# Gate and up of 19 weight tiles in two feed-forward layers: seven products of halves with sums on VectorE, in place of eight products

## The chip, the cores and the metric

The kernel runs on one core of a Trainium2 chip. The metric is the device time of one launch in microseconds (us); lower is better.

## What is computed

The reference is a diffusion backbone of two blocks over 256 context and 256 latent tokens of width 1024. Each block is a feed-forward layer, a mixer and a second feed-forward layer, so there are four feed-forward layers; the kernel's loops call them 0 to 3 by their order. The last one works on the latents alone. A feed-forward layer is, in short:

```python
def _swiglu_sub(x, mod, j, g_pre, g_post, w_in, w_out):
    h = _modulate_pre(x, g_pre, mod[:, 3 * j], mod[:, 3 * j + 1])
    gate, up = jnp.split(h @ w_in, 2, axis=-1)
    y = (jax.nn.silu(gate) * up) @ w_out
    return _gated_post(x, y, g_post, mod[:, 3 * j + 2], FFN_RES)
```

`w_in` is 1024 x 5632 (2816 columns of gate, 2816 of up), `mod` is the conditioning vector's product with `w_mod`. In the text below, "layers 2 and 3" are the second and the third feed-forward layer in the order in which they run: the last of block 0 and the first of block 1. Both work on all 512 tokens.

## The kernel before

**Numbers as two parts.** Every fp32 operand of a product is split exactly into a high part (type fp32r, made by ScalarE with a Copy) and a low part (the rest, made by VectorE with a subtraction). A product is then three matmuls: high by high, high by low, low by high. h lies in `hhi` and `hlo`, transposed, with 1024 features as eight k tiles on the partitions and the 512 tokens as columns.

**Weights.** A weight tile `f` (0 to 21) holds 128 columns of gate and 128 of up for all 1024 features: 1 MB, one DMA into one of two buffers `wraw`, then `whi` on ScalarE (L501) and `wlo` on VectorE (L502), each 128 x 2048, in three buffers each. `chunk` keeps two tiles ahead.

**The layer.** `ffn` runs the first three tiles stream by stream (`first`), since the second stream's h becomes ready later: 256 tokens at a time, gate and up in one PSUM bank (`split`). For tiles 3 to 21 (`rest`) both streams go together: 24 matmuls of 512 columns for gate, 24 for up (L656 to L658), then Silu on ScalarE (L761) and the product with up on VectorE (L762) into `act`. Behind each tile stands some modulation work (`mods`): with rate 1.75, one or two jobs, each a 512 KB load and, per stream that needs it, one pass of VectorE over 1024 columns with an accumulator (L541). Then `out_proj` multiplies `act`, split in two parts once more (L861, L862), with `w_out` in eleven chunks; its last chunks go token tile by token tile, and behind each token tile come the norms (L584 to L619) and the transposes and parts of the next layer's h (L633 to L648).

**Order.** TensorE and POOL run in the order of the program; for VectorE, ScalarE and SP (which issues the DMAs) a scheduler sets the order when the kernel is built. Every engine works through its own queue in order. `mods` puts its passes behind the last product of the tile.

Of the kernel before, what the change touches and what calls it, by code (L numbers as in the profile page):

```python
# [29 lines left out]
def rev(t):  # L30
    """128 chunk columns in the order of the backward scan: 63..0, 127..64."""
    st = t.ap[-1][0]
    return bass.AP(tensor=t.tensor, offset=t.offset + 63 * st,
                   ap=[list(x) for x in t.ap[:-1]] + [[64 * st, 2], [-st, 64]])
# [6 lines left out]
class S5Prep:  # L41
    """Discretised parameters of all 16 x 2 state groups, put down in DRAM per pair of groups."""
# [86 lines left out]
    def angles(self):  # L129
        """Everything of size [128, 16 = (dir, pair)]: first the phasors."""  # L130
# [7 lines left out]
        # phasor of one chunk, conjugated: exp(-4 i theta)  # L138
# [7 lines left out]
    def phasors(self):  # L146
        """exp(-4 i theta 2^k), k = 0..6"""
        self.steps = [self.ph]
        for k in range(1, 7):
            br, bi = self.new(), self.new()  # L150
            self.cmul(br, bi, *self.steps[k - 1], *self.steps[k - 1])
            self.unit(br, bi)
            self.steps.append((br, bi))

    def small(self, r4):
        """then the coefficients; r4 outlives the preparation"""
# [9 lines left out]
        # powers, by (pair, dir, i): forward i = power, backward i = 4 - power  # L166
# [30 lines left out]
        # input coefficients: forward j takes power 3 - j, backward j takes power j  # L197
# [8 lines left out]
    def table(self, d, q0, pool):  # L206
        """Phasor powers 0..127 of four pairs, by doubling."""
# [25 lines left out]
    def zero(self, pool):  # L233
        self.bd = pool.tile([128, 2, 2, 4, 2, 16], F32, name="s5bd", tag="s5mid", bufs=1)   # ri, dir, j, g, ch
# [4 lines left out]
    def pair(self, q, pool):  # L239
# [4 lines left out]
        B = [self.bc[:, q, :, k, :] for k in range(4)]            # [128, dir, 16]: b_re, b_im, c_re, c_im  # L244
# [27 lines left out]
    def pair_pe(self, q, pool):  # L272
# [12 lines left out]
        # by lag: the second direction's alone, both at lag 0, the first one's alone  # L285
# [19 lines left out]
class S5Main:  # L305
    """States and read-out; columns of u4 are chunks of four tokens, context first."""
# [23 lines left out]
    def fill(self, mt, ps, s=None):  # L330
        """u4 of the four pairs whose channels lie in ps [128, 512 (or one stream's 256) tokens]."""
# [94 lines left out]
# the start: feature tiles whose scale the tensor engine makes; those whose latents' scale goes by way of Pool  # L426
PE_SCALE, POOL_SCALE = 3, (3, 4, 5, 6)
# weight tile f is loaded behind the modulation of START_LOAD[f], its halves converted at feature tile 2 f, 2 f + 1
START_LOAD = (1, 3, 5)

class Kern:
# [6 lines left out]
    # ---------------------------------------------------------------- pools  # L440
# [28 lines left out]
    def ps(self, name, hold=None):  # L469
        """the next PSUM bank; hold: a set that keeps it from being given again until let() is called"""  # L470
# [11 lines left out]
    # ---------------------------------------------------------------- weights  # L482
# [3 lines left out]
    def load_upto(self, n, into=None, pieces=1, pool=False):  # L486
        """Have the n next chunks of the order on their way: raw, then its two exact parts."""
# [18 lines left out]
    def chunk(self, ahead=2):  # L506
        """The next chunk to be used."""
# [7 lines left out]
    def warm(self, f):  # L515
        """have the table of an activation function loaded"""
        self.nc.scalar.activation(self.junk_a[:, 0:1], self.mh[:, 0:1], f)

    # ---------------------------------------------------------------- modulation
# [5 lines left out]
    def mods(self, n):  # L525
        """modulation work, not before the last swiglu"""
# [25 lines left out]
    def scale_cols(self, layer, j, streams):  # L552
        """A = g_pre * (1 + scale)"""
# [6 lines left out]
    def gate_rows(self, layer, j, weight, streams):  # L560
        """weight * gate * g_post of each stream, the same row on all partitions."""
# [19 lines left out]
    # ---------------------------------------------------------------- norms  # L581
    def rstd2(self, ss):
        """ss[2] = (ss[0] + ss[1] + eps) ** -0.5"""
# [3 lines left out]
    def rstd(self, ms, n=1):  # L587
        """(ms + eps) ** -0.5 in place"""
# [4 lines left out]
    def post(self, t, y, gg, store=False):  # L593
        """x += rms(y) * gg for token tile t; y: two PSUM halves"""
# [13 lines left out]
    def pre(self, t, tag="xn"):  # L608
        """normalised token tile"""
# [12 lines left out]
    def pre_t(self, toks, layer, j):  # L622
        """h transposed, in two parts, for one or two token tiles of a stream"""
# [15 lines left out]
    def h_parts(self, p, s, k, tok, layer, j, on_vector):  # L639
        """the two parts of feature tile k of h from its transposed normalised tokens p"""  # L640
# [9 lines left out]
    # ---------------------------------------------------------------- products  # L650
    def mm_w_stat(self, out, hi, lo, col, sl):
        """out = W[:, col : col + 128].T @ h over 8 k tiles; W [128, 8, 256]"""
        nc = self.nc
        for k in range(8):
            w1, w2 = hi[:, k, col:col + 128], lo[:, k, col:col + 128]
# [4 lines left out]
    def mm_a_stat(self, outs, ahi, alo, whi, wlo, first, last):  # L660
        """outs[i] += a.T @ w[i] for one k tile; a [128, 128], w halves"""
# [7 lines left out]
    def out_proj(self, n_chunks, parts, toks, finish, tail=3):  # L669
        """token-major y = a @ W with a's k tiles on partitions; W in chunks of two k tiles.  # L670
        parts(c) -> (hi, lo) [128, 2, tokens]; the last chunks go token tile by token tile."""
# [11 lines left out]
        # the last chunks go token tile by token tile; of four tiles, the last two side by side, which  # L683
        # lets go of the chunks one by one
# [32 lines left out]
        self.bank = bank        # the banks of the first token tiles are free again first  # L717
# [4 lines left out]
    # ---------------------------------------------------------------- sub-layers  # L722
    def boundary(self, layer, j, weight, streams, nxt):
        """finish(t, y) for out_proj: post-norm of (layer, j), then the next sub-layer's pre-norm;
        nxt: (layer, j, streams), whose transposes h_ready() puts into the tensor engine's order"""
# [867 lines left out]
```

## Time and profile before

| | us |
|---|---|
| median of 3 runs | 1696.23 (1695.68 to 1696.50) |
| profiled execution, first to last instruction (the span) | 1695.7 |
| TensorE busy | 1613.1 |
| VectorE busy | 1072.1 |
| ScalarE busy | 597.6 |

The profile gives the profiled execution's span and no other time of it; it lies 0.5 us below the median of the runs. Busy time counts an engine's instructions, with overlapping ends counted once. The profile calls the engines PE (TensorE), DVE (VectorE), ACT (ScalarE), POOL and SP; PEclk is TensorE's granted clock as a share of 2.4 GHz. A line number is one of the kernel before, unless the text says that it is one of the changed kernel.

### The profile page before, as it was taken

The page shows a single profiled execution, that of the slowest core. Times are in us where ns is not written, and L with a number is a line of the kernel's source. Part 1 is how long each engine was busy: PE and PEld are TensorE (multiplying, and loading weights), DVE is VectorE, ACT ScalarE, POOL GpSimd, SP SyncE. Part 2 cuts the span into 40 slices and gives each one's busy share as a digit, 9 for nine tenths or more (in the row PEclk, how much of TensorE's full clock was granted, in tenths as well). Part 3 has the DMA queues.
Part 4 walks back from the last instruction along what each step waited for, and adds up shares of the span by engine and source line. Part 5 has one row for each costly group of instructions (what it writes and reads, how often), then busy time and mean ns, then how long its engine had stood idle before and what let it go on. Part 6 is the DMA issues. An engine that isn't in the chain of part 4 may idle for free.

```text
span 1695.7 us, 21390 instructions
## 1 busy us (share of the span) xinstructions
PE 1613.1 (95%) x8260; PEld 1358.0 (80%) x8260; DVE 1072.1 (63%) x1938; ACT 597.6 (35%) x895; POOL 268.9 (16%) x405
## 2 busy tenths in 40 slices
PE   5799959999988999999999999999999998999998
PEld 4587848888877789888888888888888877889986
DVE  6999377777657975866667465544323377665454
ACT  4431122322563444222222243222222255664342
POOL 3448800000126511000000010000000023410000
PEclk9899979999999999999999999999999999999999
DMA  7335265554342432644455422655322232135452
GB/s 307 133 125 208 90 217 183 176 218 183 119 150 97 162 136 100 224 186 186 170 180 209 162 100 105 231 186 181 112 106 99 100 115 100 63 125 199 178 208 99
DMA packets 56533, 263.93 MB, mean 156 GB/s; under 512 B 6432, under 2 KB 10992, under 8 KB 36848
## 3 DMA queue, kind: packets, MB, share of 16 engines
q1 hardware_dynamic: 56432, 262.57, 42.5%
q8 instruction: 65, 1.06, 0.2%
q14 instruction: 36, 0.29, 0.1%
HBM read 254.12 MB, written 8.43 MB: 155 GB/s over the span
## 4 chain that ended last, share of the span: by engine, by line
PE 73%; DVE 6%; POOL 3%; ACT 3%; issue 2%; POOLq 0%; DVEq 0%; ACTq 0%
PE y L667 9%; PE y L665 9%; PE y L664 9%; PE g L658 5%; PE g L656 5%; PE u L658 5%; PE g L657 5%; PE u L657 5%; PE u L656 5%; PE gu L656 3%; PE gu L658 3%; PE gu L657 3%; DVE wlo L502 1%; ACT whi L501 1%; ACT u L338 1%
## 5 line engine op out<-in xcount | busy, mean ns | idle before, releaser
L501 ACT ACTIVATE whi<-wraw 128x2048 fp32r<-128x2048 f32 (+1 forms) x155 | 285.8, 1846 | 405.7 <-PE u L657 219.7
L502 DVE TENSOR_TENSOR wlo<-wraw,whi 128x2048 fp32r<-128x2048 f32 x147 | 337.3, 2295 | 120.6 <-ACT whi L501 120.3
L541 DVE SCALAR_TENSOR_TENSOR junkv<-mraw,cond 128x1024 bf16<-128x1024 f32 x224 | 273.6, 1221 | 50.7 <-DMA mraw<-wmod 48.7
L664 PE MATMUL y<-whi,ahi 128*128 128x512 f32 x616 | 243.7, 396 | 0.0
L665 PE MATMUL y<-wlo,ahi 128*128 128x512 f32 x616 | 243.0, 394 | 0.0
L667 PE MATMUL y<-whi,alo 128*128 128x512 f32 x616 | 198.3, 395 | 0.0
L585 POOL TENSOR_TENSOR ssy<-ssy,mh 128x1 f32<-128x1 f32 x20 | 11.1, 553 | 1129.7 <-DVE ssy L584 1129.7
L658 PE MATMUL g<-hhi,wlo 128*128 128x512 f32 x456 | 179.8, 394 | 0.9 <-DVE wlo L502 0.9
L658 PE MATMUL u<-hhi,wlo 128*128 128x512 f32 x456 | 179.4, 393 | 0.0
L657 PE MATMUL g<-hlo,whi 128*128 128x512 f32 x456 | 179.1, 393 | 0.0
L657 PE MATMUL u<-hlo,whi 128*128 128x512 f32 x456 | 178.8, 392 | 0.0
L656 PE MATMUL g<-hhi,whi 128*128 128x512 f32 x456 | 178.6, 392 | 0.0
L656 PE MATMUL u<-hhi,whi 128*128 128x512 f32 x456 | 177.2, 389 | 0.0
L762 DVE TENSOR_TENSOR act<-u,act 128x512 f32<-128x512 f32 x60 | 41.4, 689 | 180.7 <-PE u L658 153.3
L657 PE MATMUL gu<-hlo,whi 128*128 128x256 f32 x496 | 139.5, 281 | 3.4 <-POOL hlo L648 3.4
L656 PE MATMUL gu<-hhi,whi 128*128 128x256 f32 x496 | 139.0, 280 | 0.0
L658 PE MATMUL gu<-hhi,wlo 128*128 128x256 f32 x496 | 138.4, 279 | 0.0
L664 PEld LDWEIGHTS y<-whi,ahi 128*128 128x128 f32 x616 | 116.1, 188 | 27.3
L665 PEld LDWEIGHTS y<-wlo,ahi 128*128 128x128 f32 x616 | 116.1, 188 | 26.9
L667 PEld LDWEIGHTS y<-whi,alo 128*128 128x128 f32 x616 | 116.0, 188 | 27.0
L862 DVE TENSOR_TENSOR alo<-act,ahi 128x1024 fp32r<-128x1024 f32 (+1 forms) x44 | 47.9, 1091 | 127.8 <-ACT ahi L861 127.2
L861 ACT ACTIVATE ahi<-act 128x1024 fp32r<-128x1024 f32 (+1 forms) x44 | 41.5, 951 | 232.8 <-PE y L665 217.2
(320 smaller groups left out, 2810.6 us busy)
## 6 DMA issues: line engine op xcount, KB each, us to landing
wraw<-wts SPq DMA_DIRECT2D x153, 1024.0 KB, 4.8
mraw<-wmod SPq DMA_DIRECT2D x133, 512.0 KB, 4.5
gg<-gg SPq DMA_DIRECT2D x10, 512.0 KB, 4.8
act<-wmod SPq DMA_DIRECT2D x8, 512.0 KB, 7.8
s5p<-dP SPq DMA_DIRECT2D x8, 384.0 KB, 5.3
dP<-s5cz SPq DMA_DIRECT2D x8, 320.0 KB, 2.3
dP<-s5st SPq DMA_DIRECT2D x8, 320.0 KB, 4.4
x<-x SPq DMA_DIRECT2D x4, 512.0 KB, 6.6
```

Of the source, the lines that this page charges most:

```text
L501: nc.scalar.activation(h, r, AF.Copy)
L502: (nc.gpsimd if pool else nc.vector).tensor_tensor(l, r, h.bitcast(F32), op=ALU.subtract)
L541: nc.vector.scalar_tensor_tensor(self.junk_v, t, 1.0, self.cond[:, s], op0=ALU.mult, op1=ALU.mult, accum_out=self.mod[:, layer, s, idx * 8 ...
L656: nc.tensor.matmul(out, w1, self.hhi[:, k, sl], start=(k == 0), stop=False)
L657: nc.tensor.matmul(out, w1, self.hlo[:, k, sl], start=False, stop=False)
L658: nc.tensor.matmul(out, w2, self.hhi[:, k, sl], start=False, stop=(k == 7))
L664: nc.tensor.matmul(o, ahi, whi[i], start=first, stop=False)
L665: nc.tensor.matmul(o, ahi, wlo[i], start=False, stop=False)
L667: nc.tensor.matmul(o, alo, whi[i], start=False, stop=last)
L762: self.mark = nc.vector.tensor_tensor(a, u, a, op=ALU.mult).ins
L861: nc.scalar.activation(hi, src, AF.Copy)
L862: nc.vector.tensor_tensor(lo, src, hi.bitcast(F32), op=ALU.subtract)
```

## The change

In layers 2 and 3 the weight tiles 3 to 21 are computed by a scheme that needs seven products of halves. The weight tile is cut into four quarters: g1, g2 (gate, features 0 to 511 and 512 to 1023) and u1, u2 (up), each 128 x 512 in memory. h is cut by features and, within each stream, by its two token tiles. Four sums of weights (s1 to s4, L492 to L494 and L508 of the changed kernel) and four differences of h (`tokens`, L462 and L469) are formed in fp32 on VectorE and then split in two parts. Each of the products p1 to p7 takes one of g1, g2, u2, s1 to s4 by 256 tokens: four k tiles by three matmuls of 256 columns. Gate of the first tokens is p1 + p2; with v = p1 + p6, gate of the others is v + p5 + p3, up of the others v + p5 + p7, and up of the first v + p7 + p4. Three PSUM banks hold a tile: p1, p6, p7 and p4 add up in one (`sa`), p5 and p3 in the second (`se`), p2 has the third (`sf`). After p1, p5 and v ScalarE copies the bank to memory; after p3, p2 and p7 VectorE adds such a copy (L575, L579, L583); Silu goes on halves, and VectorE multiplies twice (L584, and L586 after p4). p4 of a tile runs after p1 and p5 of the next.

The low parts become seven passes of 128 x 512 (L514) and the high parts seven of ScalarE (L513). The three `whi` and three `wlo` buffers become a ring of twelve slots, filled ten products ahead. The modulation work stands behind p4's product (L698 of the changed kernel). The host puts these layers' weights in the order of the quarters.

```diff
+    SEQ = (("p1", 0), ("p5", 0), ("p4", 1), ("p6", 0), ("p3", 0), ("p2", 0), ("p7", 0))
+    FORM = {"p1": "g1", "p2": "g2", "p3": "s4", "p4": "u2", "p5": "s1", "p6": "s2", "p7": "s3"}
+    SLOTS = 12
...
+    def tokens(self, s):
...
+            V.tensor_tensor(h[:, k], K.hhi[sl][:, k].bitcast(F32), K.hlo[sl][:, k].bitcast(F32),
+                                               op=ALU.add)
...
+        sub = ((t[0], b[0, 1], b[0, 0]), (t[1], b[1, 1], t[0]), (t[2], b[1, 1], b[0, 1]), (t[3], b[1, 0], t[1]))
+        for i, (o, x, y) in enumerate(sub):
+            V.tensor_tensor(o, x, y, op=ALU.subtract)
+            if i < 3:
+                self.split(i, s, o)
...
+    def load(self):
...
+        s = K.tmp.tile([128, D], F32, name="xn", tag="xn", bufs=2)
+        s1, s2 = s[:, 0:512], s[:, 512:1024]
+        V.tensor_tensor(s1, u1, u2, op=ALU.add)
+        V.tensor_tensor(s2, s1, g1, op=ALU.subtract)
+        V.tensor_tensor(u1, g1, u1, op=ALU.subtract)
...
+    def convert(self, n):
...
+        if p == "p3":
+
+            g1, g2 = forms["s2g"]
+            K.nc.vector.tensor_tensor(g1, g2, forms["s2"], op=ALU.subtract)
...
+        K.nc.scalar.activation(hi, src, AF.Copy)
+        K.nc.vector.tensor_tensor(lo, src, hi.bitcast(F32), op=ALU.subtract)
...
+        for k in range(4):
+            nc.tensor.matmul(o, w1[:, k], b1[:, k], start=(new and k == 0), stop=False, skip_group_check=not new)
+            nc.tensor.matmul(o, w1[:, k], b2[:, k], start=False, stop=False, skip_group_check=not new)
+            nc.tensor.matmul(o, w2[:, k], b1[:, k], start=False, stop=(k == 3),
+                             skip_group_check=not new)
...
+        for n, (f, p) in enumerate(self.todo):
+            self.convert(n + self.SLOTS - 2)
+            if p == "p1":
+                acc[f] = [K.ps(x)[:, 0:256] for x in ("sa", "se", "sf")]
+            a, e, g = acc[f]
+            self.product(f, p, {"p5": e, "p3": e, "p2": g}.get(p, a), p in ("p1", "p5", "p2"))
...
+            elif p == "p3":
+                t = sb[f, "u2"]
+                V.tensor_tensor(t, e, t, op=ALU.add)
+                S.activation(half(f, 1), v(t), AF.Silu)
...
+            elif p == "p7":
+                t = sb[f, "p5"]
+                V.tensor_tensor(t, a, t, op=ALU.add)
+                V.tensor_tensor(half(f, 1), v(t), half(f, 1), op=ALU.mult)
+            else:
+                K.mark = V.tensor_tensor(half(f, 0), v(a), half(f, 0), op=ALU.mult).ins
+                K.mods(K.mod_rate)
...
-            def first():
+            def first(s7):
                 w = [wv(0), wv(0)]
                 for s in range(2):
                     if s:
                         self.h_ready()
+                    s7.tokens(s)
...
-                first()
+                with tc.tile_pool(name="seven", bufs=1, reuse_waits="tile") as vp:
+                    s7 = Seven(self, vp, act)
+                    first(s7)
+                    s7.run(range(3, NF))
+                    f = NF
```

The order of VectorE's queue moves in two places. The first is a weight tile in the middle of layer 2, of which this is the kernel before, from one tile's product to the next (`mraw` is a loaded tile of `w_mod`):

```order
L762 TENSOR_TENSOR act<-u,act 128x512
L541 SCALAR_TENSOR_TENSOR junkv,mod<-mraw,cond 128x1024
L502 TENSOR_TENSOR wlo<-wraw,whi 128x2048
L541 SCALAR_TENSOR_TENSOR junkv,mod<-mraw,cond 128x1024 x3
L762 TENSOR_TENSOR act<-u,act 128x512
```

The same tile of the changed kernel, from the product with p4 on (`xn` holds the sums s1 and s2, `gg` the copies of the products):

```order
L586 TENSOR_TENSOR act<-sa,act 128x2x128
L514 TENSOR_TENSOR wlo<-wraw,whi 128x512
L698 SCALAR_TENSOR_TENSOR junkv,mod<-mraw,cond 128x1024
L514 TENSOR_TENSOR wlo<-wraw,whi 128x512
L698 SCALAR_TENSOR_TENSOR junkv,mod<-mraw,cond 128x1024
L492 TENSOR_TENSOR xn<-wraw 128x512
L698 SCALAR_TENSOR_TENSOR junkv,mod<-mraw,cond 128x1024
L493 TENSOR_TENSOR xn<-xn,wraw 128x512
L698 SCALAR_TENSOR_TENSOR junkv,mod<-mraw,cond 128x1024
L494 TENSOR_TENSOR wraw<-wraw 128x512
```

And behind these, to the next product with p4:

```order
L514 TENSOR_TENSOR wlo<-wraw,whi 128x512
L575 TENSOR_TENSOR gg<-se,gg 128x256
L514 TENSOR_TENSOR wlo<-xn,whi 128x512
L579 TENSOR_TENSOR gg<-sf,gg 128x256
L514 TENSOR_TENSOR wlo<-wraw,whi 128x512
L583 TENSOR_TENSOR gg<-sa,gg 128x256
L514 TENSOR_TENSOR wlo<-xn,whi 128x512
L584 TENSOR_TENSOR act<-gg,act 128x2x128
L508 TENSOR_TENSOR wraw<-wraw,xn 128x512
L514 TENSOR_TENSOR wlo<-wraw,whi 128x512
L586 TENSOR_TENSOR act<-sa,act 128x2x128
```

A tile's six rows of work have become twenty, and the four modulation passes stand between them.

The second place is the start of layer 2, where VectorE finishes the norms of the latents and makes the low part of the third weight tile. The kernel before, from the second tile's `wlo` on (`y` is a finished half of a token tile, `ssy` and `ssx` are its sums of squares):

```order
L502 TENSOR_TENSOR wlo<-wraw,whi 128x2048
L599 TENSOR_TENSOR y<-y,gg 128x512 x2
L584 SCALAR_TENSOR_TENSOR ssy<-ssy 128x1
L603 SCALAR_TENSOR_TENSOR x<-y,ssy,x 128x512 x2
L502 TENSOR_TENSOR wlo<-wraw,whi 128x2048
L584 SCALAR_TENSOR_TENSOR ssx<-ssx 128x1
```

The changed kernel, the twelve rows that end with the third tile's `wlo` (`act` serves as room for h and its differences, `tl` are the differences' low parts); ahead of them stand the first latent token tile's `x` and `y`, a `tl`, the second weight tile's `wlo` and the two sums of h:

```order
L469 TENSOR_TENSOR act<-act 128x4x128 x2
L741 SCALAR_TENSOR_TENSOR ssx<-ssx 128x1
L469 TENSOR_TENSOR act<-act 128x4x128
L776 TENSOR_SCALAR xn<-x,ssx 128x512 x2
L756 TENSOR_TENSOR y<-y,gg 128x512 x2
L741 SCALAR_TENSOR_TENSOR ssy<-ssy 128x1
L479 TENSOR_TENSOR tl_5208<-act,th_5207 128x4x128
L760 SCALAR_TENSOR_TENSOR x<-y,ssy,x 128x512 x2
L479 TENSOR_TENSOR tl_5210<-act,th_5209 128x4x128
L919 TENSOR_TENSOR act<-gu,act 128x256
L741 SCALAR_TENSOR_TENSOR ssx<-ssx 128x1
L659 TENSOR_TENSOR wlo<-wraw,whi 128x2048
```

The third tile's `wlo` has moved from behind the first latent tile's norm to behind the second's, and the differences stand among the norms.

## Rows read from the trace of the kernel before

**Rows 1.** Page, part 1: busy us (share of span) and instructions of an engine.

```profile
PE 1613.1 (95%) x8260; PEld 1358.0 (80%) x8260; DVE 1072.1 (63%) x1938; ACT 597.6 (35%) x895; POOL 268.9 (16%) x405
```

**Rows 2.** Busy time by stretch: layer 2's first tiles, its tiles 3 to 21, layer 3's.

```profile
core 0: us, PE busy (x) PEld busy (x) DVE busy (x) ACT busy (x) POOL busy (x), PEclk, DMA share, GB/s
634.00:675.00 41.00, 39.51 (x316) 37.87 (x315) 23.62 (x38) 19.60 (x31) 5.13 (x8) 1.00 0.26 90
675.00:884.00 209.00, 209.00 (x915) 171.40 (x914) 144.44 (x200) 50.45 (x42) 0.00 (x0) 1.00 0.51 189
...
1045.00:1254.00 209.00, 209.00 (x919) 171.64 (x918) 93.88 (x106) 51.00 (x42) 0.00 (x0) 1.00 0.48 171
```

**Rows 3.** Timeline of PE in layer 2 (start, us), and Silu in tile g's view.

```profile
699.66 0.39 PE L656 MATMUL g<-hhi,whi 128*128 128x512 f32 x1
...
711.78 0.39 PE L658 MATMUL g<-hhi,wlo 128*128 128x512 f32 x1
...
L761 ACT ACTIVATE act<-g x19: 598/598/601, 679.3 to 877.0; 128x512 f32<-128x512 f32 x19
```

**Rows 4.** Timeline of PE in layer 2's first tiles, 256 columns.

```profile
639.76 0.28 PE L656 MATMUL gu<-hhi,whi 128*128 128x256 f32 x1
...
645.89 0.28 PE L657 MATMUL gu<-hlo,whi 128*128 128x256 f32 x1
```

**Rows 5.** Timeline of DVE in layer 2: starts and durations of its passes.

```profile
709.55 2.29 DVE L502 TENSOR_TENSOR wlo<-wraw,whi 128x2048 fp32r<-128x2048 f32 x1
711.75 0.16 DVE L545 TENSOR_TENSOR mod<-mod,cols 128x8 f32<-128x8 f32 x1
...
715.42 1.22 DVE L541 SCALAR_TENSOR_TENSOR junkv<-mraw,cond 128x1024 bf16<-128x1024 f32 x1
...
716.68 1.22 DVE L541 SCALAR_TENSOR_TENSOR junkv<-mraw,cond 128x1024 bf16<-128x1024 f32 x1
717.83 0.08 DVE L541 DVE_READ_ACCUMULATOR junkv<-mraw,cond 128x1 f32 x1
717.83 0.69 DVE L762 TENSOR_TENSOR act<-u,act 128x512 f32<-128x512 f32 x1
718.43 1.22 DVE L541 SCALAR_TENSOR_TENSOR junkv<-mraw,cond 128x1024 bf16<-128x1024 f32 x1
```

**Rows 6.** Timeline of DVE: a 256-wide pass and its successor.

```profile
677.79 0.42 DVE L762 TENSOR_TENSOR act<-gu,act 128x256 f32<-128x256 f32 x1
678.12 1.22 DVE L541 SCALAR_TENSOR_TENSOR junkv<-mraw,cond 128x1024 bf16<-128x1024 f32 x1
```

**Rows 7.** Busy time of line L541 alone: tiles 3 to 21 of layers 2, 3.

```profile
675.00:880.00 205.00, 88.42 (x144) 1.00 0.51 191
...
1045.00:1250.00 205.00, 36.79 (x60) 1.00 0.48 170
```

**Rows 8.** Layer 2's first tiles: timelines of DVE and ACT, and tile gu's view.

```profile
638.25 2.28 DVE L502 TENSOR_TENSOR wlo<-wraw,whi 128x2048 fp32r<-128x2048 f32 x1
...
643.48 1.41 DVE L603 SCALAR_TENSOR_TENSOR x<-y,ssy,x 128x512 f32<-128x512 f32 x2 [0.66 <-POOL ssy L585]
...
646.65 0.88 DVE L619 TENSOR_SCALAR xn<-x,ssx 128x512 f32<-128x512 f32 x2 [0.66 <-POOL ssx L585]
...
662.33 1.91 ACT L501 ACTIVATE whi<-wraw 128x2048 fp32r<-128x2048 f32 x1 [4.68 <-PE gu L657]
...
L656 PE MATMUL gu<-hhi,whi x496: 276/280/367, 634.8 to 1627.0; 128*128 128x256 f32 x166
```

**Rows 9.** A gap of PE in the mixer ahead: timeline, and stretches with PEclk.

```profile
485.19 0.39 PE L934 MATMUL v<-whi,hhi 128*128 128x256 f32 x1 [2.46 <-ACT u L338]
...
485.92 0.41 PE L936 MATMUL v<-whi,hlo 128*128 128x256 f32 x1
...
489.31 0.28 PE L934 MATMUL v<-whi,hhi 128*128 128x256 f32 x1
...
487.00:488.00 1.00, 1.00 (x6) 0.50 0.00 0
```

**Rows 10.** ACT's 512-wide conversion (line L861) and the weight loads (page, part 6).

```profile
L861 ACT ACTIVATE ahi<-act x44: 612/1060/1062, 330.5 to 1671.8; 128x1024 fp32r<-128x1024 f32 x33, 128x512 fp32r<-128x512 f32 x11
...
wraw<-wts SPq DMA_DIRECT2D x153, 1024.0 KB, 4.8
```

More of the change, by code (lines that the diff above doesn't have):

```diff
@@ L654, in mm_w_stat @@
         for k in range(8):
-            w1, w2 = hi[:, k, col:col + 128], lo[:, k, col:col + 128]
+            w1, w2 = (z[:, col // 128, k] if len(z.shape) == 4 else z[:, k, col:col + 128] for z in (hi, lo))
             nc.tensor.matmul(out, w1, self.hhi[:, k, sl], start=(k == 0), stop=False)
@@ L771, in wv @@
             def wv(ahead=2):
+                if both and not extra:
+                    return [p.rearrange("p (i k n) -> p i k n", i=2, k=8) for p in self.chunk(ahead)]
                 return [p.rearrange("p (k n) -> p k n", k=8) for p in self.chunk(ahead)]
-            def first():
+            def first(s7):
                 w = [wv(0), wv(0)]
@@ L863, in new_parts @@
                     return hi, lo
+                if f == NF:
+                    ready = {c: new_parts(c) for c in range(2)}
                 while f < NF:
@@ L1544, in host @@
         for n in range(NF):
-            put(i * CH_FFN + n, w1, range(8), np.r_[n * 128:n * 128 + 128, FF + n * 128:FF + n * 128 + 128])
+            c = i * CH_FFN + n
+            put(c, w1, range(8), np.r_[n * 128:n * 128 + 128, FF + n * 128:FF + n * 128 + 128])
+            if i in (1, 2):
+                wts[c] = wts[c].reshape(128, 8, 2, 128).transpose(0, 2, 1, 3).reshape(128, 2048)
         for n in range(NF // 2):
```

85 lines of the change are left out of this document (added).

## The prediction

> **What bounds the kernel now.** I read the page's busy shares first: TensorE is busy 95% of the span, VectorE 63% [rows 1]. The second view is the busy time by stage: in weight tiles 3 to 21 of layers 2 and 3 TensorE has no idle time at all (209.00 of 209.00), while VectorE is busy 144 us in layer 2 and 94 in layer 3 [rows 2]. So these stretches last as long as their matmuls. The third view is the spacing of matmuls, since a matmul's listed 0.39 us overlaps the next one: 12.12 us hold 53 starts of 512 columns, 0.2287 us each. 48 of them make 10.98 us, and the 18 steps between the first and the last Silu of the stretch give the same 10.98 [rows 3]. With 256 columns 6.13 us hold 52 starts, 0.1179 each, 3% over half [rows 4].
>
> So a tile costs TensorE 10.98 us now and 7 x 12 x 0.1179 = 9.90 us after: 1.08 less, 41 us over 2 x 19 tiles, if TensorE stays the bound. The question is whether VectorE then fits into 9.9 us.
>
> **VectorE's price of a tile.** Its passes overlap at their ends too, so I take start to start: the 2048-wide pass 2.20 us, the 512-wide 0.60, the 1024-wide modulation pass 1.15 ahead of another kind and 1.26 ahead of its like [rows 5], the 256-wide 0.33 [rows 6]. Gone from a tile are one 2048-wide pass and one 512-wide product: 2.8 us. New are 11 passes of 512 (four sums of weights, seven low parts) and five of 256 (three sums, two products): 11 x 0.60 + 5 x 0.33 = 8.25 us. The modulations stay where they were: 1.75 jobs a tile, one pass per stream. In layer 2 that is 3.5 passes: 144 records are 72 passes, each with its accumulator read [rows 7]. In layer 3 only the latents are left and the jobs run out after 30 passes (60 records). In the new order the passes alternate with others, so 1.15 each: 4.0 us a tile in layer 2, 2.0 in the first 14 tiles of layer 3.
>
> Layer 2 therefore asks 12.3 us of VectorE per tile against 9.9 of TensorE: **VectorE becomes the bound**. Layer 3 asks 10.3 in 14 tiles and 8.25 in five, where TensorE sets 9.9. The ten halves converted ahead don't help for long: p4 adds into the bank that holds p7, so TensorE stops ahead of p4 until VectorE has taken p7's sum, and that sum stands in VectorE's queue among the later halves. TensorE can be ahead by p1 and p5 only, and its idle time will stand before p4.
>
> The Trainium skill, VectorE: DVE Perf Modes, section The DRAIN you can't avoid, says that the next pass does not start until the pipeline of the one before has emptied. The rows disagree: a pass of 0.69 us is followed after 0.60 [rows 5]. By that rule a tile of layer 2 would cost 2.0 us more and the sum would be the third rival's.
>
> **Layer 2, summed over its queue.** From the last part of the second stream's h to the p7 sum of tile 20 the order holds 217 passes of 512 (one 1024-wide counted twice), 91 of 256, 70 modulation passes and a few narrow ones: 217 x 0.60 + 91 x 0.33 + 70 x 1.15 + 0.8 = 241.5 us. Let T be the moment when TensorE has finished the first weight tile for the second stream, 662.3 now [rows 8]. That queue starts about 3.2 us before T (the 24 matmuls of up, 2.8, and a hand-over). After it TensorE still runs p4, p6, p3, p2, p7 and p4, 6 x 1.41 us, with 0.9 of hand-overs (estimate): 9.4. The stretch then ends at T + 247.7. Now it ends at T + 2 x 5.65 + 19 x 10.98 = T + 219.9. That is 28 more.
>
> To this come waits inside the queue. VectorE does 2.0 us of work between the p7 sum and the product with p4; p4 at full clock needs 1.41 and two hand-overs, so there is no wait. At half clock p4 needs twice that and VectorE waits about 1.1 us; between none and 20 us over 18 tiles. After TensorE had been idle for 2.46 us its clock was granted at 0.50, the lower of the two levels, 0.7 us after it started again, for 3 us [rows 9]; the new gap of about 2.4 us before each p4 is of that length. I take a quarter, 5 us, because such a clock falls partly behind p4. For other hand-overs and for late weight loads (4.8 us to land [rows 10], with some 6 us between the release of a raw tile and its first sum) I take 4, between 0 and 20. Layer 2's tiles: 28 + 9 = 37 us more.
>
> **The first three tiles of both layers.** VectorE now sums h, forms four differences and splits three of them per stream: 2 x 1.13 + 4 x 0.60 + 3 x 0.60 = 6.5 us (1.13 from the 512 and the 2048 passes). In the order they stand between the parts of h and the next norms, and the third tile's wlo, which started at 638.25, now stands just ahead of the second tile's xn, which started at 646.65. That moment becomes 646.65 - 2.20 + 6.5 less what falls into waits of the norm for POOL and ScalarE; I take 2.4 of it; bounds are none and the four waits of 0.66, 2.6. So wlo is ready at about 650.8, and TensorE wants it at 634.8 + 2 x 5.65 + 0.24 = 646.35 [rows 8]: 4.5 us. The half clock behind such a gap costs 1.6 (3.2 us at half speed [rows 9]). In the second stream 0.60 + 1.13 + 0.60 us stand ahead of the last part of h, for which TensorE already waits: 2.3. Together 8.4 us per layer.
>
> **Layer 3, the same way.** 217 x 0.60 + 92 x 0.33 + 30 x 1.15 + 3 = 198 us of queue. Where the modulations have run out TensorE sets the pace, and VectorE idles 2.3 x 1.65 in tiles 18 to 20 and 8.25 in each of the last two, which have nothing left to convert, less a 2.20 pass for the output's weights: 18. With p4 at the end, 1.9, the end is T - 3.2 + 198 + 18 + 1.9 = T + 214.7, against 219.9: 5 less. Hand-overs give back 2, the first tiles cost 8.4, and one alo stands behind the last product, 1. Layer 3: 6 more.
>
> **Costs of nothing.** ScalarE makes seven conversions of at most 0.61 us [rows 10] and five narrower passes, under 7.4 us of a tile's 9.9. The output's first weights take the second ring tile, free after p4 of tile 20; their 1.9 + 2.2 us lie under p6, p3, p2 and p7 (5.6); without that cover they would cost 4 a layer. The rows of gates are loaded later, since the sums use their tiles, but are wanted only after eight chunks of the output. On SP's queue the weight loads stand behind modulation loads that wait for passes that are earlier in VectorE's queue anyway.
>
> **Sum.** The profiled execution's span is 1695.7 us, 0.5 below the median of the runs. 37 + 8.4 + 6 = 51 us more: **1747 us**.
>
> **Rivals.**
> *TensorE stays the bound (faster).* For it speaks that VectorE idles 37% of the span. It decides at 9.9 us of VectorE per tile: in layer 2 the 512-wide pass would have to take (9.9 - 4.0 - 1.65) / 11 = 0.39 us, and no two-input row does. Then 41 us go and the first tiles cost 0 to 17: 1655 to 1671. Chance 0.04.
> *The clock falls before each p4 of layer 2.* Then p4 costs VectorE the whole 1.1 us a tile, 15 us above my sum, and the falls in layer 3's smaller gaps (about 0.5 us) some more: 1762 to 1770. For it speaks that 2.46 us of idling were enough [rows 9]; against it that a slower TensorE also fills the gap that makes it slow. In a sentence beside it: the Trainium skill, TensorE: Matmul & The Clock Gate, section HAM oscillation, describes a kernel that loses the high clock again at every wait between short bursts; the row agrees that one wait does it. Chance 0.18.
> *The passes don't overlap where each waits for a semaphore.* Whole durations of 0.69, 0.42 and 1.30 add 11 x 0.09 + 5 x 0.09 + 3.5 x 0.15 = 2.0 us a tile in layer 2 and 1.7 in 14 tiles of layer 3, 60 us: 1805. Against it are rows 5, where passes that wait for ScalarE follow early too. Chance 0.06.
> *The first tiles hide their part.* 17 us less: 1730. Chance 0.12.
>
> **Numbers.** My forecast has 0.60. The range from 1724 to 1779 takes in the fourth rival with the low bounds of the waits, and the second with their high ones; it leaves out the first, the third and some of the tails. Told apart can be 0.2%, 3.4 us: faster 0.05, within it 0.01, slower 0.94.
>
> **What would show it.** In layer 2's stretch VectorE should be busy nearly all the time and TensorE some 80%, with a period of 12.3 to 13 us where two jobs' passes stand and its idle time before p4, released by the sum after p7 (L583 of the changed kernel); in layer 3's last tiles the period should be 9.9. The third tile's wlo should release TensorE once per layer after 4 to 5 us. The output stretches should be unchanged. I am wrong if layer 2's tiles take 9.9 us with VectorE waiting, or if the time sits in loads or in ScalarE.

## The result, and the profile after

The changed kernel takes 1750.43 us (median of 4 runs, 1748.67 to 1754.40) against 1696.37 for the kernel before (1695.68 to 1697.01): ratio 1.0323, 95% interval 1.0308 to 1.0337. It is slower by 54 us. The span of its profiled execution is 1747.5 us, 51.8 longer than before; the two medians lie 54.1 apart. The stretches below are those of the two profiled executions.

First the page: busy time by engine and the chain that ended last, by engine and by line (L numbers here are the changed kernel's).

```profile
PE 1605.0 (92%) x9628; PEld 1417.5 (81%) x9628; DVE 1304.1 (75%) x2510; ACT 731.1 (42%) x1291; POOL 278.2 (16%) x405
...
PE 51%; DVE 24%; issue 4%; ACT 3%; POOL 3%; DMA 1%; DVEq 0%; POOLq 0%; ACTq 0%; SPq 0%
```

VectorE has 232 us more to do than before, TensorE 8 less [rows 1], and a quarter of the chain now runs over VectorE. Next the busy time by stretch; the borders are TensorE's first matmul of a layer, of its tile 3, and of its output, from the timeline.

```profile
core 0: us, PE busy (x) PEld busy (x) DVE busy (x) ACT busy (x) POOL busy (x), PEclk, DMA share, GB/s
632.30:682.50 50.20, 42.69 (x305) 40.97 (x304) 39.76 (x69) 21.98 (x44) 9.30 (x8) 0.86 0.12 43
682.50:926.40 243.90, 203.15 (x1598) 199.77 (x1597) 235.73 (x449) 110.60 (x224) 0.00 (x0) 0.94 0.49 161
1051.00:1102.00 51.00, 43.17 (x305) 41.57 (x304) 39.77 (x70) 20.69 (x43) 8.94 (x8) 0.87 0.12 42
1102.00:1304.00 202.00, 193.54 (x1600) 190.60 (x1598) 187.99 (x356) 110.21 (x225) 0.00 (x0) 0.99 0.52 178
```

In layer 2's tiles 3 to 21 the two engines have changed places: VectorE is busy 97% of the time and TensorE 83%; before it was 69% and 100% [rows 2]. With the same borders the span's 51.8 us come from these places:

| stretch | before | after | difference |
|---|---|---|---|
| start of the program to layer 2 | 634.82 | 632.34 | -2.5 |
| layer 2, first three tiles | 38.73 | 50.20 | +11.5 |
| layer 2, tiles 3 to 21 | 208.79 | 243.91 | +35.1 |
| output of layer 2 | 124.54 | 124.52 | 0.0 |
| layer 3, first three tiles | 38.96 | 51.07 | +12.1 |
| layer 3, tiles 3 to 21 | 208.79 | 201.95 | -6.8 |
| output of layer 3 to the end | 441.07 | 443.51 | +2.4 |

Of the -2.5, 1.7 arose in the first 50 us and the rest by 320 us; the change touches neither. What TensorE waited for in layer 2, and what VectorE waited for in its tiles (us in total, times, longest):

```profile
PE sa L530 <- DVE gg L583: 40.7, 16, 9.3
PE gu L815 <- DVE wlo L659: 4.6, 1, 4.6
PE gu L814 <- POOL hlo L805: 1.9, 3, 0.8
PE gu L814 <- DVE hlo L805: 1.0, 1, 1.0
```

```profile
DVE act L586 <- PE sa L532: 6.7, 7, 1.1
```

The first row is the bank of p4, released by the sum behind p7. The period is the step from one such sum to the next on VectorE's timeline, in layer 2 first and then in the last tiles of layer 3:

```profile
716.12 0.41 DVE L583 TENSOR_TENSOR gg<-sa,gg 128x256 f32<-128x256 f32 x1
...
726.85 0.41 DVE L583 TENSOR_TENSOR gg<-sa,gg 128x256 f32<-128x256 f32 x1
...
739.72 0.41 DVE L583 TENSOR_TENSOR gg<-sa,gg 128x256 f32<-128x256 f32 x1
...
752.59 0.41 DVE L583 TENSOR_TENSOR gg<-sa,gg 128x256 f32<-128x256 f32 x1
756.09 0.42 DVE L586 TENSOR_TENSOR act<-sa,act 128x256 f32<-128x256 f32 x1 [0.96 <-PE sa L532]
...
1291.23 0.42 DVE L583 TENSOR_TENSOR gg<-sa,gg 128x256 f32<-128x256 f32 x1 [1.00 <-PE sa L532]
...
1301.14 0.43 DVE L583 TENSOR_TENSOR gg<-sa,gg 128x256 f32<-128x256 f32 x1 [0.88 <-PE sa L532]
```

10.73 us stand between two sums with two modulation passes, 12.87 where there are four; no such pass stands between the last two rows: 9.91, and VectorE waits for TensorE. Last, the price of a pass, from VectorE's timeline in layer 2:

```profile
710.76 1.22 DVE L698 SCALAR_TENSOR_TENSOR junkv<-mraw,cond 128x1024 bf16<-128x1024 f32 x1
711.90 0.08 DVE L698 DVE_READ_ACCUMULATOR junkv<-mraw,cond 128x1 f32 x1
711.90 0.68 DVE L494 TENSOR_TENSOR wraw<-wraw 128x512 f32<-128x512 f32 x1
...
713.65 0.69 DVE L514 TENSOR_TENSOR wlo<-wraw,whi 128x512 fp32r<-128x512 f32 x1
714.26 0.41 DVE L575 TENSOR_TENSOR gg<-se,gg 128x256 f32<-128x256 f32 x1
714.59 0.68 DVE L514 TENSOR_TENSOR wlo<-xn,whi 128x512 fp32r<-128x512 f32 x1
```

From start to start 1.14 us for a modulation pass, 0.61 for one of 512 columns, 0.33 for one of 256.

### The profile page after: what moved, and what is told of

It is laid out like the page before. It is cut to its first block, busy times and chain, and to the rows that moved or that the text cites. A ratio compares the mean times of both kernels' runs of the same rounds, so it can differ in the third digit from the quotient of the medians.

```text
span 1747.5 us, 25201 instructions
## 1 busy us (share of the span) xinstructions
PE 1605.0 (92%) x9628; PEld 1417.5 (81%) x9628; DVE 1304.1 (75%) x2510; ACT 731.1 (42%) x1291; POOL 278.2 (16%) x405
## 4 chain that ended last, share of the span: by engine, by line
PE 51%; DVE 24%; issue 4%; ACT 3%; POOL 3%; DMA 1%; DVEq 0%; POOLq 0%; ACTq 0%; SPq 0%
PE y L824 8%; PE y L821 8%; PE y L822 8%; DVE junkv L698 6%; DVE wlo L514 5%; PE gu L814 3%; PE gu L815 3%; PE gu L813 3%; DVE wlo L659 2%; PE sa L530 2%; PE sa L531 1%; PE sa L532 1%; ACT whi L658 1%; DVE xn L492 1%; DVE xn L493 1%
## 5 line engine op out<-in xcount | busy, mean ns | idle before, releaser
L659 DVE TENSOR_TENSOR wlo<-wraw,whi 128x2048 fp32r<-128x2048 f32 x109 | 250.5, 2298 | 100.0 <-ACT whi L658 99.7
L698 DVE SCALAR_TENSOR_TENSOR junkv<-mraw,cond 128x1024 bf16<-128x1024 f32 x224 | 273.0, 1219 | 42.4 <-DMA mraw<-wmod 41.5
L658 ACT ACTIVATE whi<-wraw 128x2048 fp32r<-128x2048 f32 (+1 forms) x117 | 212.9, 1822 | 215.7 <-DMA wraw<-wts 86.0
L513 ACT ACTIVATE whi<-wraw 128x512 fp32r<-128x512 f32 x190 | 115.7, 627 | 111.7 <-DVE wraw L508 48.5
L814 PE MATMUL gu<-hlo,whi 128*128 128x256 f32 x496 | 145.0, 292 | 6.2 <-POOL hlo L805 4.0
L530 PE MATMUL sa<-hhi,whi 128*128 128x256 f32 x304 | 92.3, 304 | 48.6 <-DVE gg L583 48.6
L514 DVE TENSOR_TENSOR wlo<-wraw,whi 128x512 fp32r<-128x512 f32 x190 | 128.4, 681 | 1.2 <-ACT whi L513 1.0
L815 PEld LDWEIGHTS gu<-hhi,wlo 128*128 128x128 f32 x496 | 98.0, 198 | 9.6 <-DVE wlo L659 9.6
L814 PEld LDWEIGHTS gu<-hlo,whi 128*128 128x128 f32 x496 | 98.1, 198 | 9.1 <-POOL hlo L805 5.7
L530 PEld LDWEIGHTS sa<-hhi,whi 128*128 128x128 f32 x304 | 60.8, 200 | 54.7 <-DVE gg L583 54.6
L813 PEld LDWEIGHTS gu<-hhi,whi 128*128 128x128 f32 x496 | 98.4, 198 | 0.1
```

Source lines behind the costliest of these rows:

```text
L513: K.nc.scalar.activation(hi, src, AF.Copy)
L514: K.nc.vector.tensor_tensor(lo, src, hi.bitcast(F32), op=ALU.subtract)
L530: nc.tensor.matmul(o, w1[:, k], b1[:, k], start=(new and k == 0), stop=False, skip_group_check=not new)
L658: nc.scalar.activation(h, r, AF.Copy)
L659: (nc.gpsimd if pool else nc.vector).tensor_tensor(l, r, h.bitcast(F32), op=ALU.subtract)
L698: nc.vector.scalar_tensor_tensor(self.junk_v, t, 1.0, self.cond[:, s], op0=ALU.mult, op1=ALU.mult, accum_out=self.mod[:, layer, s, idx * 8 ...
```

## The experiments

Two theories stood at the start. Theory Q is the prediction's: VectorE's queue sets the tiles of layer 2 and the first three tiles cost by themselves. Theory W puts the loss on the waits ahead of p4, so that a better place for p4 would give it back. The stretches named below have the borders of the table. All ratios are to the kernel before.

### Seven products in layer 3 alone

```diff
+            elif both and which:
+                first(None)
             elif both:
                 with tc.tile_pool(name="seven", bufs=1, reuse_waits="tile") as vp:
...
-            if i in (1, 2):
+            if i == 2:
```

(`first(None)` leaves `tokens` out, and the layer goes on with eight products; the reading of its weights is set back too.)

> Layer 2 is computed by eight products again, layer 3 stays with seven. Theory Q (VectorE's queue sets the tiles of layer 2, the first three tiles of each layer cost by themselves): layer 2 gives back its 46.6 us (11.5 in the first tiles, 35.1 in the others), layer 3 keeps its own 12.1 in the first tiles, its 4.9 to 6.8 us of gain in the others and 2.0 at the output's start; 1704 us, between 1699 and 1709. Theory W (the loss comes with the waits ahead of p4, 16 in layer 2 and 12 in layer 3): three sevenths of the loss stay, 1717 to 1723 us.

1704.7 us (1.0048, 1.0033 to 1.0063), as Q expected. Layer 2 is back at 38.73 and 208.79 us; layer 3 takes 49.73 and 203.32. So the two layers add up. Even alone in layer 3, where VectorE fits better, the sevens lose: 5.5 us are gained in the tiles and 10.8 lost ahead of them.

### Narrow modulation passes

```diff
-            nc.vector.scalar_tensor_tensor(self.junk_v, t, 1.0, self.cond[:, s], ...
+            w = 64 if self.narrow else D
+            nc.vector.scalar_tensor_tensor(self.junk_v[:, 0:w], t[:, 0:w], 1.0, self.cond[:, s, 0:w], ...
```

(`narrow` is set around the passes that stand behind p4.)

> The modulation passes that stand behind tiles 3 to 21 of layers 2 and 3 multiply 64 of 1024 columns, so their sums leave out the rest; their loads, their number and their place in every queue stay. Theory Q: a pass falls from 1.15 to about 0.2 us (estimate, from the 0.08 us of the accumulator's read and the 0.15 us of the narrowest sums), VectorE asks 8.25 + 3.5 x 0.2 = 9.0 us of a layer 2 tile, TensorE's 9.9 is the bound: layer 2's tiles 3 to 21 go from 243.9 us to 195 to 205, layer 3's from 202.0 to 193 to 200; the time is 1700 to 1710 us. Theory W: the sums still stand between p7 and p4, so most waits ahead of p4 stay: 1735 to 1750 us.

1725.56 us (1.0170, 1.0152 to 1.0188), between the two expectations. Layer 3's tiles take 198.4 us, as expected by Q; layer 2's take 222.0, 22 less than with full passes but 17 to 27 more than I expected. VectorE's waits in layer 2 name what came in their place:

```profile
DVE xn L492 <- DMA wraw<-wts: 31.5, 15, 3.6
```

Now that VectorE is ahead, the first sum of a tile waits for the tile's weights in 15 of 19 tiles, 2.1 us on average. Theory W has fallen, since the waits ahead of p4 shrank from 40.7 to 15.0 us without p4 being moved; but Q was short of a next limit.

### p4 three products' time later

```diff
-    SEQ = (("p1", 0), ("p5", 0), ("p4", 1), ("p6", 0), ("p3", 0), ("p2", 0), ("p7", 0))
+    SEQ = (("p1", 0), ("p5", 0), ("p6", 0), ("p3", 0), ("p4", 1), ("p2", 0), ("p7", 0))
```

> p4 of the tile before runs behind p1, p5, p6 and p3 instead of behind p1 and p5, 2.8 us of TensorE's work later. Theory Q: VectorE has as much to do as before; TensorE stands still as long, only elsewhere. What can go is VectorE's own waiting for p4 (10.2 us in 9 waits) and the low clock behind the gaps: 1738 to 1750 us. Theory W: p7's sum has 2.8 us more, over half of the 48.6 us of waits ahead of p4 go: 1710 to 1725 us.

1759.3 us (1.0367, 1.0343 to 1.0390): slower by another 9, which neither theory expected; layer 2's tiles take 249.3 us, layer 3's 208.2. In layer 2 TensorE waits about as long as before, and VectorE has a wait of its own:

```profile
PE sa L530 <- DVE gg L583: 39.8, 18, 5.6
```

```profile
DVE wlo L514 <- ACT whi L513: 9.4, 8, 2.0
```

Theory W wanted over half of the 40.7 us to go; 0.9 went. That the stall stays where VectorE's work stays is Q's reading. The new loss lies in layer 2 in VectorE's waits for ScalarE's high parts, in layer 3 in TensorE's waits for ScalarE's copies (6.8 us) and VectorE's for weights (8.1); layer 2's output takes 4.3 us longer too, 2.4 of it a wait for the first `alo` (the low part of `act`). Why these come late in this order wasn't tried.

### The sums of weights on POOL

```diff
-        V.tensor_tensor(s1, u1, u2, op=ALU.add)
-        V.tensor_tensor(s2, s1, g1, op=ALU.subtract)
-        V.tensor_tensor(u1, g1, u1, op=ALU.subtract)
+        P = nc.gpsimd
+        P.tensor_tensor(s1, u1, u2, op=ALU.add)
+        P.tensor_tensor(s2, s1, g1, op=ALU.subtract)
+        P.tensor_tensor(u1, g1, u1, op=ALU.subtract)
...
-            K.nc.vector.tensor_tensor(g1, g2, forms["s2"], op=ALU.subtract)
+            K.nc.gpsimd.tensor_tensor(g1, g2, forms["s2"], op=ALU.subtract)
```

> The four sums of weights s1 to s4 of each tile run on POOL, which has nothing to do in these stretches. Theory Q: VectorE's queue per tile falls by 4 x 0.60 = 2.4 us, to 9.9 us in layer 2 and 7.9 in layer 3; POOL needs about 4 x 1.3 = 5.2 us a tile (its 128 x 512 passes elsewhere take 1.31). Layer 2's tiles 3 to 21 then take 200 to 215 us, layer 3's 193 to 200: 1702 to 1718 us. Rival C: POOL and VectorE hinder each other at memory, each POOL pass lengthens the VectorE passes beside it by its own time: 12.3 - 2.4 + 5.2 = 15.1 us a tile, 1780 us or more. Rival L: POOL's sums come late, since its slower passes stand in one chain, and TensorE waits for weights: 1725 to 1750 us.

1814.04 us (1.0695, 1.0679 to 1.0710): rival C, and Q's expectation was wrong by about 100 us. Layer 2's tiles take 276.8 us, layer 3's 233.6. VectorE's and POOL's timelines in layer 2, beside each other:

```profile
768.68 1.82 POOL L493 TENSOR_TENSOR xn<-wraw 128x512 f32<-128x512 f32 x1 [6.41 <-DMA wraw<-wts]
769.27 2.31 DVE L699 SCALAR_TENSOR_TENSOR junkv<-mraw,cond 128x1024 bf16<-128x1024 f32 x1
770.58 2.15 POOL L494 TENSOR_TENSOR xn<-xn,wraw 128x512 f32<-128x512 f32 x1
...
771.52 0.41 DVE L576 TENSOR_TENSOR gg<-se,gg 128x256 f32<-128x256 f32 x1
771.85 1.96 DVE L699 SCALAR_TENSOR_TENSOR junkv<-mraw,cond 128x1024 bf16<-128x1024 f32 x1
772.70 2.27 POOL L495 TENSOR_TENSOR wraw<-wraw 128x512 f32<-128x512 f32 x1
...
773.75 1.76 DVE L515 TENSOR_TENSOR wlo<-wraw,whi 128x512 fp32r<-128x512 f32 x1
...
778.57 0.68 DVE L515 TENSOR_TENSOR wlo<-wraw,whi 128x512 fp32r<-128x512 f32 x1
```

Beside a POOL pass a VectorE pass of 0.68 us takes 1.76 and a modulation pass of 1.22 takes 1.96 to 2.31, and POOL's own passes take about 2 us where they took 1.31 elsewhere. The pass that reads one operand from PSUM (L576) keeps its 0.41 in the middle of it. VectorE is busy 258.6 us in layer 2's tiles, 23 more than in the changed kernel, though four passes a tile have left it. So POOL's idle time is of no use here to passes with both operands in SBUF. The Trainium skill, SBUF — State Buffer, section SBUF: two separate sides, says the same: VectorE with two SBUF inputs and a POOL operation that reads SBUF take a shared pair of ports in turn. By that rule rival C should have been my expectation.

### Sums of h later

```diff
-                    s7.tokens(s)
                     for f in range(3):
...
                         split(f, w[f], slice(256 * s, 256 * s + 256))
+                    with tc.issue_after(self.mark_hv if s else self.mark_lo):
+                        s7.tokens(s)
```

(`mark_lo` is the last low part of weights, `mark_hv` the last high part of h on VectorE.)

> The sums and differences of h stand in VectorE's queue behind the third tile's wlo (first stream) and behind the last part of the second stream's h. The first tiles lost 11.5 us in layer 2 and 12.1 in layer 3: 4.6 of waiting for that wlo, 2.5 of half clock behind it, 4.8 of the second stream's h and its half clock. Theory Q, taken strictly: layer 3, where VectorE is not full to the end, gets back 5 to 11 us; in layer 2 VectorE is full from the second stream's h to the end, and what the first tiles give back (7 to 11) comes again as waiting in tile 3, except what VectorE now does in the 10.4 us in which it was idle there: 1734 to 1744 us. Rival F (the first tiles' loss is TensorE's alone and simply goes, in both layers): 1728 to 1732 us. Rival S (the sums are late now where p5 of tile 3 wants them, as late as they were early): 1746 to 1754 us.

1738.17 us (1.0246, 1.0229 to 1.0263), in Q's range of 1734 to 1744. The first tiles take 43.65 us in layer 2 and 41.97 in layer 3, 6.6 and 9.1 less; tiles 3 to 21 take 244.07 and 202.72, as good as before. The wait for the third tile's wlo is gone. What the first tiles gave back in layer 2 did not come again in tile 3: VectorE did the sums in time in which it had been idle: it is busy 40.0 of the 43.65 us there, where it was busy 39.8 of 50.2.

### Modulations moved, and both edits

```diff
-                K.mods(K.mod_rate)
+                K.mods(K.seven_rate)
...
+    seven_rate = 0.5
...
-                self.mods(3 * self.mod_rate)
+                self.mods(3 * self.seven_rate)
...
-                self.mod_rate = 2.5 if extra else 1.75
+                self.mod_rate = 3 if extra else 2
...
-            self.mod_rate = 1.2
+            self.mod_rate = 1.6
```

> Tiles 3 to 21 of layers 2 and 3 get 0.5 modulation jobs each instead of 1.75; the rest moves to the first layer's tiles (1.6 jobs instead of 1.2), its output (3 instead of 2.5) and the outputs of layers 2 and 3 (2 instead of 1.75). Nothing is left out. Theory Q: VectorE asks 8.25 + 0.5 x 2 x 1.15 = 9.4 us a tile, TensorE's 9.9 is the bound in both layers: layer 2's tiles 3 to 21 take 200 to 212 us instead of 243.9, layer 3's 196 to 200 instead of 202.0; elsewhere 0 to 5 us more: 1703 to 1718 us. Rival D (weight loads are late as soon as VectorE is not, as with the narrow passes, whatever the modulations' loads do): layer 2's tiles take about 222 us: 1722 to 1730 us.

1706.23 us (1.0052, 1.0037 to 1.0066), in Q's range. VectorE's work falls to 176 us; these are layer 2's tiles 3 to 21:

```profile
694.70:886.00 191.30, 189.86 (x1599) 188.56 (x1597) 175.66 (x333) 110.38 (x225) 0.00 (x0) 1.00 0.39 138
```

TensorE is the bound again, busy 189.9 of 191.3 us at full clock, 17 us below the eight products and even below my 200 to 212. Layer 3's tiles take 194.2 us. Rival D has fallen: with fewer modulation loads on the way VectorE's list of waits there has none for weights.

> Both edits: modulations moved, sums of h later. Theory Q: with VectorE below TensorE in both layers the first tiles' part now comes back in both, 10 to 20 us below the modulations alone: 1685 to 1705 us. If the sums of h, the first conversions and tile 3's p5 stand in each other's way: 1705 to 1720 us. Below 1694 us it would beat the kernel before.

This kernel has the edits of the last two diffs. 1692.46 us (0.9972, 0.9961 to 0.9983), faster than the kernel before by 0.28%. First tiles 43.90 and 43.97, tiles 3 to 21 191.67 and 192.28. So by the profiles the tiles 3 to 21 of both layers win 33.6 us over the kernel before, and all but 1.2 are lost elsewhere: 12.1 ahead of layer 2, 10.2 in the first tiles and 10.1 in the two outputs, whose matmuls wait 2.8 us each for their first `alo`.

> The kernel before (eight products) with the same moved modulations, as a control: TensorE has no idle time in tiles 3 to 21 there, so the rates of modulation should change nothing: 1695 to 1700 us. If it is faster by over 0.2%, what the moved modulations give to the changed kernel is not due to VectorE's part in the sevens alone.

1708.07 us (1.0067, 1.0051 to 1.0083), outside my 1695 to 1700. The move itself costs 11 us with eight products, and 9.4 of the profile's 10.2 lie ahead of layer 2. In the first layer TensorE waits longer for low parts that stand behind modulations in VectorE's queue: 10.6 us up to 200 us after the start, where the kernel before has 0.7.

```profile
PE g L658 <- DVE wlo L502: 10.6, 3, 7.5
```

So against the same plan of modulations the sevens with both edits are worth 15.6 us (1708.07 - 1692.46).

### Other places for the modulations

```diff
-                    self.mods(self.mod_rate)
+                    self.mods(1.9 if extra and f >= 10 else self.mod_rate)
```

> The version with both edits, but the first layer takes its extra modulations only from tile 10 on (1.9 jobs a tile there, 1.2 before), since the control with eight products lost 11 us, of them 12 by the first layer's tiles at 160 to 195 us, where VectorE is full. Theory: layers 2 and 3 keep their 191.7 and 192.3 us, the first layer gives back 6 to 11 us: 1681 to 1687 us. If the loss moves along with the modulations: 1690 to 1696 us.

1687.97 us (0.9951, 0.9938 to 0.9964), just above the 1681 to 1687 expected: the best kernel of the study, 8.7 us below the median of the kernel before in these runs, 1696.66. The first layer gave back less than I hoped: its one long wait for the tables of S5, a part of the mixer, 15.3 us with both edits and 19.6 in the kernel before, is now 26.3, while its waits for low parts fell from 8.9 to 0.8.

```profile
PE wbt L281 <- DVE s5bd L267: 26.3, 1, 26.3
```

By the profiles 2.8 of the 5.4 us gained over both edits lie ahead of layer 2. Layer 2's tiles lose 2.5 (194.2 us) and its output wins 4.9, where the wait for the first `alo` is gone; why that part comes in time now wasn't tried.

The other place was layers 2 and 3 themselves (0.85 jobs a tile; the first layer's tiles at 1.2):

> The version with both edits, but the first layer's tiles keep 1.2 jobs and layers 2 and 3 take 0.85 a tile. VectorE then asks 8.25 + 0.85 x 2 x 1.15 = 10.2 us of a layer 2 tile, 0.3 above TensorE's 9.9. Theory Q: layer 2's tiles take 2 to 8 us more than 191.7, layer 3's, with fewer passes from the middle on, 0 to 4 more, and the first layer's 8 to 11 come back: 1683 to 1695 us.

1698.08 us (1.0012, 1.0003 to 1.0021), a miss by 3 us. Layer 2's tiles take 200.64 us, 9 more than with 0.5 jobs. VectorE is busy 191.6 of them. By my sum it was asked for 0.3 us a tile more than TensorE; the tiles took 0.5 us longer each.

### TensorE kept busy ahead of p4

```diff
+            if p == "p4" and K.which7:
+                o = K.ps("dm")[:, 0:256].rearrange("p (s n) -> p s n", s=2)
+                w, b = self.parts[f, p][0], self.moving(p)[0]
+                for k in range(12):
+                    nc.tensor.matmul(o, w[:, k % 4], b[:, k % 4], start=(k == 0), stop=(k == 11))
```

(`which7` is true in layer 2.)

> The changed kernel, and in layer 2 twelve matmuls of 256 columns (1.41 us) into a PSUM bank that nobody reads stand ahead of each p4, so that TensorE's idle time there falls from about 2.4 to 1 us; nothing else changes. If VectorE's waits for p4 (10.2 us in 9 waits) come from the half clock behind these gaps, they go, and the granted clock of layer 2's tiles is 1.00: 1738 to 1746 us. If the clock there costs nothing, since VectorE is the bound: 1748 to 1753 us. If the added matmuls stand in the way of p4: 1756 us and more.

1746.44 us (1.0294, 1.0281 to 1.0308), 4.0 below the changed kernel, though single runs of the two overlap. Two stretches of its layer 2's tiles:

```profile
720.00:765.00 45.00, 41.60 (x348) 40.98 (x347) 44.71 (x86) 22.57 (x46) 0.00 (x0) 1.00 0.46 153
765.00:810.00 45.00, 42.86 (x358) 42.45 (x359) 45.00 (x87) 20.47 (x41) 0.00 (x0) 1.00 0.46 160
```

The granted clock is 1.00 there, VectorE has next to no idle time, and its waits for p4 are one of 2.5 us in place of seven of 6.7 in all; layer 2's tiles take 240.8 us instead of 243.9. So the half clock ahead of p4 is real, and worth about 3 us of the 54. The rest of the 4.0 can't be put down to it: in this profile layer 3's first tiles, which the edit leaves alone, take 2.9 us less as well.

## Why the prediction was right, by its steps

**VectorE's price.** Right within 0.01 us: 0.60 to 0.61, 0.33 and 1.14 us from start to start, behind waits too. That settles the third rival: no pass waited for the one before to end. Beside it, the prediction gave only half of what the Trainium skill says: in VectorE: DVE Perf Modes, section The DRAIN you can't avoid, the rule is followed by the remark that a next operation which is not held starts earlier. The rows agree with the remark, 0.60 us against a listed 0.68.

**Layer 2, tiles 3 to 21.** 37 us were predicted, 35.1 came. The 5 us for half clock ahead of p4 are borne out by 6.7 us of VectorE's waits and by the run with TensorE kept busy. VectorE's other waits came to 1.3 us, where I had put 4. The clock fell ahead of some of the p4s only: VectorE waited for seven in 18, about a third of the 20 us that the second rival would have cost, where I had taken a quarter. The length of TensorE's wait alone doesn't tell which, as these two p4s show:

```profile
740.19 0.39 PE L530 MATMUL sa<-hhi,whi 128*128 128x256 f32 x1 [2.73 <-DVE gg L583]
740.41 0.28 PE L531 MATMUL sa<-hlo,whi 128*128 128x256 f32 x1
...
753.05 0.58 PE L530 MATMUL sa<-hhi,whi 128*128 128x256 f32 x1 [2.73 <-DVE gg L583]
753.43 0.42 PE L531 MATMUL sa<-hlo,whi 128*128 128x256 f32 x1
```

Both follow a wait of 2.73 us. Behind the first the granted clock is 1.00 and p4 takes 1.5 us, behind the second it is 0.50 and p4 takes 2.7.

**The first three tiles.** The step that was off: 8.4 us predicted, 11.5 and 12.1 measured. The wait for the third wlo is 4.6 us, as the order had told (4.5). Off was the term for the half clock. These are TensorE's waits, and the clock behind them, in layer 2:

```profile
648.61 0.58 PE L815 MATMUL gu<-hhi,wlo 128*128 128x256 f32 x1 [4.57 <-DVE wlo L659]
...
663.71 0.46 PE L814 MATMUL gu<-hlo,whi 128*128 128x256 f32 x1 [1.00 <-DVE hlo L805]
665.30 0.58 PE L814 MATMUL gu<-hlo,whi 128*128 128x256 f32 x1 [0.69 <-POOL hlo L805]
```

```profile
648.60:656.40 7.80, 7.79 (x47) 7.79 (x48) 1.79 (x4) 0.63 (x1) 0.36 (x1) 0.68 0.37 134
...
662.00:668.00 6.00, 4.31 (x19) 3.72 (x19) 6.00 (x11) 1.65 (x3) 1.35 (x2) 0.66 0.00 1
668.00:676.00 8.00, 8.00 (x60) 8.00 (x59) 5.91 (x11) 3.10 (x6) 0.00 (x0) 0.83 0.01 2
```

Behind the first wait a clock of 0.68 over 7.8 us costs 2.5 (7.8 x 0.32) instead of my 1.6. In the second stream I had counted 2.3 us of late h and no clock. The waits grew by only 1.4 us, from 1.5 to 2.9 in all, but the clock fell once more: 6.0 x 0.34 + 8.0 x 0.17 = 3.4. The four terms give 11.9, slightly over the 11.5, since TensorE stood still for some of the time at the low clock.

**Layer 3, tiles 3 to 21.** 5 less, 2 back for hand-overs and 1 for an alo were predicted. Measured are 6.8 less and 1.9 more at the output's start, of which 1.7 is the wait for the alo. The 2 for hand-overs didn't come.

**The sum.** 46.6 + 7.2 - 2.5 (the start) + 0.5 = 51.8 against 51 predicted: the first tiles were sized 6.8 too low, the other tiles of both layers 4.8 too high, and the start, on which nothing rests, made up most of the rest. That the spans agree within 1 us is luck, since these errors cancel; the median, 1750.43, lies 3.4 above the 1747 that I forecast. The mechanism, VectorE's queue in layer 2, is no luck: its rows and the run with moved modulations show it.

**The rivals.** TensorE as the bound: excluded here by VectorE's 97%, and brought about in the run with moved modulations, where the tiles take 191.4 and 194.2 us, near the 188 of the matmuls alone. First tiles that hide their part: excluded, though with another place in the queue they hide over half of it. What I had as a cost of nothing, the weight loads, did cost next to nothing here (0.3 us of VectorE's waits in layer 2's tiles), but 31.5 us of waits in the run with narrow passes, where VectorE is ahead.

## What to carry to other kernels

Fewer matmuls pay only as far as the engine that prepares their operands keeps up: sum its queue over a whole stretch, side work included, before counting the matmuls saved. When it doesn't fit, look first for side work in the stretch that can be done elsewhere (here the modulations), and measure that move by itself in the old kernel, since it can cost where it arrives. An idle engine isn't free help if it shares a path to memory with the busy one.

## What the runs showed that I had not expected

- Two SBUF operands on POOL and on VectorE at the same time: of VectorE's 512-wide passes in layer 2's tiles the 39 beside a POOL pass took 1.54 us on average, the 86 others 0.68; passes with a PSUM operand kept their 0.41 us.
- Four waits of TensorE of 0.4 to 1.0 us within 7 us went along with a granted clock of 0.66; until then I had seen such a fall only behind a single wait of 2.46 us [rows 9]. And of two single waits of 2.73 us one kept the full clock.
- Where VectorE was relieved, the next limit stood close behind: 2.1 us of waiting for weights per tile with all modulation loads on the way, none with fewer of them.
